# A macaron transformer block on one Trainium2 core: the product with w_o by two sets of seven block products, x read back in two lots, one load pool for all stages

## The chip, the cores and the metric

One NeuronCore of one Trainium2 chip runs the whole kernel in one launch. The metric is the device time in microseconds; the time before is the median of three runs, 1166.94 us (1165.9 to 1168.38). All operands are fp32, 512 tokens by 1024 features.

## The reference, cut to what matters

The block is two feed-forward networks with a mixer between them; the change is in the last lines of the mixer.

```python
x = x + 0.5 * swiglu(rmsnorm(x, g1), ffn1_w_gu, ffn1_w_down)
x = x + hybrid_mixer(rmsnorm(x, gm), ...)
x = x + 0.5 * swiglu(rmsnorm(x, g2), ffn2_w_gu, ffn2_w_down)
return rmsnorm(x, final_norm_g)

# the end of hybrid_mixer
y_conv = (cb * causal_short_conv(cc * cu, conv_w)) @ w_out_conv    # 1024 x 1024
y_gla = (o * silu(r)) @ w_out_gla                                  # 1024 x 1024
merged = sigmoid(ga) * y_conv + sigmoid(gb) * y_gla
return merged @ w_o                                                # 1024 x 1024
```

## The kernel before, in words

**Layout.** Activations are held transposed: eight tiles of 128 features by 512 tokens. TensorE takes a 128 x 128 block of a weight matrix as the loaded operand and streams 512 or 256 tokens past it. An fp32 product is made of three passes in the type fp32r: high part of the weight by high part of the activation, high by low, low by high. The high part is a cast, the low part what is left of the value after subtracting the cast.

**Weights.** `Weights` walks a table. `PLAN` lists every block of every weight matrix in the order in which it lies in DRAM; `STEPS` lists what TensorE does with it, step by step. A block of 128 x 1024 values is loaded by SyncE (`dma`, L334) into one of ten load slots `f`; `until` notes the step after which a slot is free. For each step, ScalarE casts the block into `wh` (L374) and VectorE subtracts into `wl` (L375); there are three buffers of each, and a step's cast and subtraction are issued two steps ahead of its matmuls, so the cast of step k waits for the buffer that the matmuls of step k-3 read.

**Sets of seven products.** Wide matrices are not multiplied block by block. A 2 x 2 arrangement of blocks is done with seven products in place of eight, by sums and differences of blocks on both sides (as Strassen's method does). The products are named m1, p2, q6, p5, q7, p4, p3. Each takes one sum of weight blocks and one sum of activation blocks: 24 matmuls of 128 x 256 on TensorE (L533, class `Product`, `narrow`). The sums of weight blocks are made in the load slots: VectorE adds one (L361), and the others are added by GpSimd DMAs that add into their target (L352, `add`). The first of these, a11 += a21, is issued when m1's low part is done, the second, a12 += a11, when p2's is. `sets` puts the blocks of a matrix into `PLAN` and the order of the products into `STEPS`; where two sets follow each other, `order` interleaves them: 0:m1 p2 q6 p5 q7, 1:m1, 0:p4 p3, 1:q6 p5 q7 p2 p4 p3. The sums of the activation side (`Operands`) are VectorE operations of 128 x 1024 in place (L749 to L756); each operand is then split by ScalarE casts (L623) and VectorE subtractions (L624) into two `op` tiles, of which there are 14. `run_sets` asks for operands two steps ahead.

**Accumulation.** A set needs three PSUM banks, a, b and c. Bank b is read after m1, q6 and q7, into a tile or another bank (ScalarE, L579 and L583), and is accumulated into further. When a quarter of the output is complete (p2, q7, p4, p3), VectorE takes it out: for w_out_gla, it is multiplied by a gate (L1641) and added to the merged tiles y (L1645).

**The stage of the change.** After w_out_conv (eight plain units, one of eight 128-column stripes each) comes w_out_gla, two sets, 14 products, 336 matmuls of 128 x 256. Then the four merged y tiles are split (L1560 and L1561, four times, 128 x 1024 each), and w_o is multiplied plainly: four steps that make four stripes at once (`mm_group`, L423, 96 matmuls of 128 x 512), then four single stripes (`mm_single`, L409, 96 more). `evac` adds each stripe to the old x (L1662, eight of 128 x 512) and starts that stripe's part of the next norm (L459 to L469). The old x was written to DRAM earlier; eight SyncE DMAs (L1623) read it back during w_out_conv into tiles that are free by then, and the sum goes into the tile X2. FFN2 follows with plain steps.

**Order.** All of the code is written in one sequence and a scheduler places each engine's instructions; what stands in each engine's list is what the engine runs, in that order. PSUM banks of the pool `mm` are handed out in turn; `AUX` is a bank apart.

Of the kernel before, what the change touches and what calls it, by code (L numbers as in the profile page):

```python
# [8 lines left out]
F32 = mybir.dt.float32  # L9
# [6 lines left out]
P = 128  # L16
# [55 lines left out]

HW = 256


# [104 lines left out]
def block_kernel(ctx: ExitStack, tc: tile.TileContext, xT, vecs, gf, gup, wgl, wts, out):  # L180
# [98 lines left out]
    for n, b in (("wh", 3), ("wl", 3), ("op", 14)):  # L279
        pools[n] = ctx.enter_context(tc.tile_pool(name=n, bufs=b))  # L280
    acc_row = ctx.enter_context(tc.tile_pool(name="acc_row", bufs=1))
    class Weights:

        def __init__(self, ahead):
            self.ahead = ahead
            self.issued = 0
            self.taken = 0
            self.end = 0  # L290
            self.ready = []
            self.raw = {}
            self.loads = {}
            self.sums = {}
            self.first = {}

        def phase(self, early, first=6):


            self.early = early  # L300
            self.until = [-1] * SLOTS
# [27 lines left out]
        def dma(self, n, until):  # L329
            u = PLAN[n]  # L330
            w = unit_cols(u)
            o = offset(n)
            t = self.slot(until)
            nc.sync.dma_start(t[:, :w], wts[o : o + P * w].rearrange("(p n) -> p n", p=P))  # L334
            return t

        def load_set(self, n):

            a = {p: STEPS.index((n, p)) for p in SEQ}
            for i in range(self.issued, a["m1"]):  # L340
                if STEPS[i][1] is None and STEPS[i][0] not in self.raw:
                    self.raw[STEPS[i][0]] = self.dma(STEPS[i][0], i)
            a21 = self.dma(n + 2, max(a["p5"], a["m1"] + 3))
            a11 = self.dma(n, a["p2"] + 3)
            a22 = self.dma(n + 3, a["p4"])
            s3 = self.slot(a["q7"])
            a12 = self.dma(n + 1, a["p3"])
            self.raw[n] = [a11, a12, a21, a22, s3]
# [5 lines left out]
        def issue(self):  # L354
# [192 lines left out]
    class Set:  # L547
# [52 lines left out]
        def quarter(self, p):  # L600
# [12 lines left out]
            return t  # L613

    class Both:

# [113 lines left out]
    class Operands:  # L730
# [4 lines left out]

        def __init__(self, b):
            self.b = b
            self.parts = {}
            self.sums = set()
# [20 lines left out]
        def make(self, p):  # L760
            if p in self.parts:
                return
            i = self.ORDER.index(p)
            if i > 0:
                self.make(self.ORDER[i - 1])
            v = self.sum(p)
# [377 lines left out]
    def mixer(norm, nxt):  # L1144
# [8 lines left out]

        Y = [tile_of("y", [P, 2, S + 2]) for _ in range(4)]

# [422 lines left out]
        def sigmoid(t):  # L1578
# [3 lines left out]

        c_h, c_l = parts([Y[i][:, :, 2:] for i in range(4)])
        m = [two(d // 2)[:, d % 2] for d in range(KD)]

# [9 lines left out]
        ga = [gate("ga", d) for d in range(2)]  # L1595
        x_old = [QK[2 + i][:, j] for i in range(2) for j in range(2)] + [
            pools["g"].tile([P, S], F32, tag=t, name=f"{t}_x") for t in ("sc", "reset", "gup_w", "glr")]
        gb_new = []
# [5 lines left out]
        for d in range(KD):  # L1604
# [16 lines left out]
            if d in AT:  # L1621
                oo.make(AT[d])
            nc.sync.dma_start(x_old[d], xs[d])  # L1623
            if d < 4:
# [4 lines left out]
        sigmoid(gb_new.pop())  # L1629
        m_h, m_l = [None] * KD, [None] * KD  # L1630

        def gla_done(i):
            def done(s, p):
                if not (i == 1 and p in ("q6", "p5", "q7")):
                    finish_late()
                if p not in QUARTERS:
# [6 lines left out]
                    op0=ALU.mult, op1=ALU.mult)  # L1643
                y = two(d // 2)
# [12 lines left out]

        run_sets(lambda i: Set(oo, gla_done(i)), hooks={(0, "p3"): [reload]})
        finish_late()
# [5 lines left out]
        for d, o in enumerate(mm_group("w_o", KD, (0, P, 2 * P, 3 * P), m_h, m_l)):  # L1665
            evac(d, o)
        for d in range(4, KD - 2):
            evac(d, mm_single("w_o", KD, d * P, m_h, m_l))
        for d, o in [(d, mm_single("w_o", KD, d * P, m_h, m_l)) for d in range(KD - 2, KD)]:
            evac(d, o)  # L1670

    FFN = dict(f=1, hidw=2, hid=3, tp=9)
    with phase("small1", **FFN):
# [10 lines left out]
        ffn("ffn1_w_gu", "ffn1_w_down", n1, nm, PLAIN1, 5)  # L1684
    with phase("small2", f=1, v=4, qk=2, g=1, y=4, small=1):
        W.phase(4, 5)
# [49 lines left out]
```

## Time and profile before

| what | value |
|---|---|
| median of three runs | 1166.94 us |
| the profiled execution's own time | 1166.18 us |
| its span in the trace | 1164.1 us |
| granted TensorE clock | 0.999 |
| TensorE matmul, busy | 1155.0 us in 6626 matmuls |
| VectorE, busy | 956.7 us in 1198 instructions |
| ScalarE, busy | 684.6 us in 904 instructions |
| GpSimd, busy | 117.7 us in 153 instructions |

How to read it: `PE` is TensorE's matmul row, `PEld` its weight loads, `DVE` VectorE, `ACT` ScalarE, `POOL` GpSimd and `SP` SyncE. A busy PE row is not a measure of throughput, since matmuls overlap each other: the time of one matmul is read from the distance between starts. In the timeline a row gives the start, the length, the line, output<-inputs, the shape and the count. The first 366 us are FFN1, the mixer follows to 823 us (w_out_gla from 739.14 us, w_o from 779.67 us), and FFN2 is the rest.

### The profile page before, as it was taken

How to read it: one execution, taken by the hardware profiler on the slowest of the kernel's cores; microseconds unless marked ns; L12 is line 12 of the kernel's file. 1: busy time of each engine (PE TensorE's matmuls, PEld its weight loads, DVE VectorE, ACT ScalarE, POOL GpSimd, SP SyncE). 2: the span in 40 equal slices, each digit the busy share in tenths (PEclk: the TensorE clock that was granted, in tenths of full speed). 3: DMA queues.
4: the chain of work that ended last, by engine and by line, in shares of the span. 5: the costliest groups of instructions: out<-in, count | busy, mean ns of one | idle time of the engine just before them, and what ended most of it. 6: DMA issues, size and time to landing. Idle time of an engine off the chain costs nothing.

```text
span 1164.1 us, 17143 instructions
## 1 busy us (share of the span) xinstructions
PE 1155.0 (99%) x6626; PEld 1016.1 (87%) x6626; DVE 956.7 (82%) x1198; ACT 684.6 (59%) x904; POOL 117.7 (10%) x153
## 2 busy tenths in 40 slices
PE   9999999999999999999999999999999999999997
PEld 7898888988888889999989998998889888898886
DVE  7997888997568977979799998686599788889955
ACT  6466666675335656666666586544356666666443
POOL 0010111101020111100101100000001111111100
PEclk9999999999999999999999999999999999999999
DMA  9388787678524488876868767531738777757721
GB/s 350 79 212 195 178 201 180 163 193 204 207 80 122 106 200 230 197 188 171 224 169 207 211 171 221 134 107 52 227 74 209 182 187 177 196 145 183 184 86 73
DMA packets 62593, 200.11 MB, mean 172 GB/s; under 512 B 6864, under 2 KB 13136, under 8 KB 62512
## 3 DMA queue, kind: packets, MB, share of 16 engines
q1 hardware_dynamic: 39088, 126.37, 32.3%
q0 software_dynamic: 18784, 68.17, 31.8%
q10 hardware_dynamic: 4640, 4.49, 1.1%
q8 instruction: 52, 0.85, 0.3%
q14 instruction: 29, 0.24, 0.1%
HBM read 124.55 MB, written 8.39 MB: 114 GB/s over the span
## 4 chain that ended last, share of the span: by engine, by line
PE 96%; DVE 2%; ACT 1%; DMA 1%; issue 1%; ACTq 0%
PE mm L824 13%; PE mm L409 11%; PE mm L533 11%; PE bb L542 10%; PE z L542 8%; PE mm L423 8%; PE w L542 7%; PE y L542 6%; PE mm L1041 4%; PE aux L824 4%; PE x L542 3%; PE y L533 3%; PE w L533 2%; PE aux L1041 1%; PE z L533 1%; PE x L533 1%
## 5 line engine op out<-in xcount | busy, mean ns | idle before, releaser
L374 ACT CAST wh<-f 128x1024 fp32r<-128x1024 f32 (+1 forms) x341 | 356.0, 1047 | 339.6 <-PE mm L533 37.8
L375 DVE TENSOR_TENSOR wl<-f,wh 128x1024 fp32r<-128x1024 f32 (+1 forms) x341 | 413.6, 1217 | 98.4 <-ACT wh L374 89.3
L352 POOL DMA_DIRECT2D f<-f x126 | 109.0, 865 | 905.8 <-DVE wl L375 512.0
L824 PE MATMUL mm<-wh,op 128*128 128x512 f32 x432 | 106.9, 389 | 0.0
L533 PE MATMUL mm<-op,wh 128*128 128x256 f32 x800 | 105.6, 284 | 0.0
L533 PEld LDWEIGHTS mm<-op,wh 128*128 128x128 f32 x800 | 100.1, 192 | 0.5 <-ACT tp L583 0.2
L542 PE MATMUL bb<-op,wh 128*128 128x512 f32 x384 | 97.9, 395 | 0.0
L824 PEld LDWEIGHTS mm<-wh,op 128*128 128x128 f32 x432 | 80.9, 188 | 16.7
L409 PE MATMUL mm<-op,wh 128*128 128x512 f32 x384 | 91.0, 389 | 0.0
L409 PEld LDWEIGHTS mm<-op,wh 128*128 128x128 f32 x384 | 72.0, 188 | 15.0
L542 PEld LDWEIGHTS bb<-op,wh 128*128 128x128 f32 x384 | 69.4, 189 | 12.7
L542 PE MATMUL z<-op,wh 128*128 128x512 f32 x256 | 64.4, 393 | 0.0
L423 PE MATMUL mm<-op,wh 128*128 128x512 f32 x256 | 64.1, 392 | 0.2 <-DVE op L456 0.2
L824 PE MATMUL mm<-wl,op 128*128 128x512 f32 x216 | 57.7, 389 | 0.0
L423 PEld LDWEIGHTS mm<-op,wh 128*128 128x128 f32 x256 | 47.5, 188 | 10.9 <-ACT wh L374 0.5
L542 PEld LDWEIGHTS bb<-op,wl 128*128 128x128 f32 x384 | 52.3, 190 | 5.0 <-DVE wl L375 1.3
L533 PE MATMUL mm<-op,wl 128*128 128x256 f32 x400 | 56.5, 283 | 0.0
L542 PE MATMUL w<-op,wh 128*128 128x512 f32 x224 | 56.3, 393 | 0.0
L542 PE MATMUL bb<-op,wl 128*128 128x256 f32 x384 | 53.6, 282 | 0.9 <-DVE wl L375 0.9
L542 PEld LDWEIGHTS z<-op,wh 128*128 128x128 f32 x256 | 46.0, 189 | 8.2
L361 DVE TENSOR_TENSOR f<-f,f 128x1024 f32<-128x1024 f32 x42 | 51.3, 1222 | 1.6 <-DMA f<-wts 0.9
L533 PEld LDWEIGHTS mm<-op,wl 128*128 128x128 f32 x400 | 51.8, 192 | 0.3
(334 smaller groups left out, 2003.7 us busy)
## 6 DMA issues: line engine op xcount, KB each, us to landing
f<-wts SPq DMA_DIRECT2D x219, 512.0 KB, 4.5
f<-f POOLq DMA_DIRECT2D x126, 512.0 KB, 5.2
X<-xT SPq DMA_DIRECT2D x8, 256.0 KB, 5.4
xs<-X POOLq DMA_DIRECT2D x8, 256.0 KB, 2.4
tp<-ga SPq DMA_DIRECT2D x8, 256.0 KB, 5.6
y<-tp SPq DMA_DIRECT2D x7, 256.0 KB, 2.0
ga<-tp ACTq DMA_DIRECT2D x6, 256.0 KB, 3.9
gb<-tp ACTq DMA_DIRECT2D x6, 256.0 KB, 3.9
```

The lines of the kernel that those rows point to most:

```text
L352: return nc.gpsimd.dma_start(out_, a, accum_op=ALU.add).ins
L361: nc.vector.tensor_tensor(out=s3, in0=a11, in1=a21, op=ALU.add)
L374: self.cast = nc.scalar.copy(h[:, :w], raw[:, :w]).ins
L375: nc.vector.tensor_tensor(out=l[:, :w], in0=raw[:, :w], in1=h[:, :w].bitcast(F32), op=ALU.subtract)
L409: nc.tensor.matmul(o, w[:, i * P : (i + 1) * P], a[k], start=j == k == 0, stop=j == 2 and k == kt - 1)
L423: nc.tensor.matmul(o[c], w[:, s : s + P], a[k], start=k == 0 and j == 0, stop=k == kt - 1 and j == 2)
L533: nc.tensor.matmul(o[:, e * HW : (e + 1) * HW], w[:, k * HW + e * P : k * HW + (e + 1) * P], a(k), start=self.fresh and j == k == e == 0, ...
L542: nc.tensor.matmul(o[:, e, :n], w[:, k * HW + e * P : k * HW + (e + 1) * P], a(k), start=self.fresh and k == 0 and w is self.h, stop=k == ...
L824: nc.tensor.matmul(o[t], a(k)[:, t * P : (t + 1) * P], ww[:, i * 512 : (i + 1) * 512], start=fresh and j == k == 0, stop=j == 2 and k == 3 ...
L1041: nc.tensor.matmul(o[t][e], b if j == 1 else a, wl if j == 2 else wh, start=k == K0 and e == 1 and j == 0, stop=k == KF - 1 and j == 2, sk ...
```

## The change

1. **w_o becomes two sets** of seven products, 2 x 7 x 24 = 336 matmuls of 128 x 256, done by a new class `Straight`. It accumulates into banks a, b, c without reading b out in between, except for one ScalarE copy of bank b into bank a after m1. The plain units, the four splits of y and the eight `evac` additions go. Each set's products come in the order of `OUT_SEQ`; those of w_out_gla in that of `GLA_SEQ`, which differs from before in one place: p2 of the second set comes two products earlier, so that q7 and p4 of that set follow each other directly.
2. **The activation side of w_o** is made by `Operands` over the merged tiles, now one tile `YS` that the view `MY` covers: seven operands, each two casts and two subtractions of 128 x 512, and four sums of 128 x 1024.
3. **The weight sums of w_o.** The third sum, a11 + a21, is not made by VectorE: a11 is loaded a second time and a GpSimd DMA adds a21 to it straight from DRAM (`BY_DMA`). For the second set the sums are placed one step ahead of m1, not three.
4. **x is read back into X2 itself** by eight ScalarE DMAs in two lots of four (`read_back`), and each finished quarter is added in place, by twelve VectorE operations of 128 x 2 x 256.
5. **The load pool `f`** is made once and kept through all stages, and `until` with it.

```diff
+BY_DMA = ("w_o",)
...
+GLA_SEQ = ((0, "m1"), (0, "p2"), (0, "q6"), (0, "p5"), (0, "q7"), (1, "m1"), (0, "p4"),
...
-def sets(mat, pairs):
+def sets(mat, pairs, seq=None):
...
-    STEPS.extend(order(firsts))
+    STEPS.extend([(firsts[i], p) for i, p in seq] if seq else order(firsts))
...
-    sets("w_out_gla", [(4 * i * P, (4 * i + 2) * P) for i in range(2)])
-    units(group("w_o", KD, (0, P, 2 * P, 3 * P)))
-    for d in range(4, KD):
-        units(single("w_o", KD, d * P))
+    sets("w_out_gla", [(4 * i * P, (4 * i + 2) * P) for i in range(2)], GLA_SEQ)
+    sets("w_o", [(4 * i * P, (4 * i + 2) * P) for i in range(2)], OUT_SEQ)
...
+    pools["f"] = ctx.enter_context(tc.tile_pool(name="f", bufs=1, reuse_waits="tile"))
...
-                    self.sums.setdefault(max(lo + 3, i - 3), []).append(n)
+                    ahead = 1 if (PLAN[n][0], STEPS[i - 1][1]) == ("w_o", "q6") else 3
+                    self.sums.setdefault(max(lo + 3, i - ahead), []).append(n)
...
-            s3 = self.slot(a["q7"])
+            s3 = self.dma(n, a["q7"]) if PLAN[n][0] in BY_DMA else self.slot(a["q7"])
...
-                nc.vector.tensor_tensor(out=s3, in0=a11, in1=a21, op=ALU.add)
+                if PLAN[n][0] not in BY_DMA:
+                    nc.vector.tensor_tensor(out=s3, in0=a11, in1=a21, op=ALU.add)
                 self.first[n] = self.add(a21, a22)
+                if PLAN[n][0] in BY_DMA:
+                    self.add(s3, self.block(n + 2))
...
+    class Straight:
...
+        def run(self, p):
+            n = self.BANK[p]
+            fresh = n not in self.bank
+            if fresh:
+                self.bank[n] = self.new(n)
+            Product(*W.take(), self.group.get(p), fresh).narrow(self.bank[n])
+            if p == "m1":
+                self.bank["a"] = self.new("a")
+                nc.scalar.copy(self.bank["a"], self.bank["b"])
+            self.done(p, self.bank[n])
...
-            nc.sync.dma_start(x_old[d], xs[d])
...
-                if p in ("p4", "p3"):
-                    def f():
-                        for j, (b, c) in enumerate(split_pair(y)):
-                            m_h[d + j], m_l[d + j] = b, c
-                    late.append(f)
...
-        def evac(d, o):
-            nc.vector.tensor_tensor(out=x[d], in0=o, in1=x_old[d], op=ALU.add)
-            nxt.add(d)
...
+        def read_back(ks):
+            for d in ks:
+                nc.scalar.dma_start(x[d], xs[d])
...
+        mo = Operands(
+            lambda j, l: MY[:, 4 * j : 4 * j + 4, half(l)],
+            ("m1", "p2", "p5", "q6", "q7", "p3", "p4"))
+
+        def out_done(i):
+            def done(p, o):
+                if p == "m1":
+                    return
+                a = int(p in ("p5", "q7", "p4"))
+                l = int(p not in ("p2", "p4"))
+                d = 4 * i + 2 * a
+                v = XS[-1][:, d : d + 2, half(l)]
+                if a:
+                    nc.vector.scalar_tensor_tensor(out=v, in0=pair(o), scalar=-1.0, in1=v,
+                                                   op0=ALU.mult, op1=ALU.add)
+                else:
+                    nc.vector.tensor_tensor(out=v, in0=pair(o), in1=v, op=ALU.add)
+                for k in NORMS.get((i, p), ()):
+                    nxt.add(k)
+            return done
...
+        def out_bank(i):
+            return lambda n: AUX() if (i, n) == (1, "b") else MM()
...
+        run_sets(out_set, hooks={
+            (0, "p3"): [reload], (1, "q6"): [lambda: read_back(range(0, 4))],
+            (1, "p4"): [lambda: read_back(range(4, KD))]})
```

The scheduler turns this into other lists. **The first place is the end of w_out_gla on TensorE.** Before, the last two products of w_out_gla (p4 into one bank, p3 into another) are followed by the first group of w_o:

```order
L533 MATMUL mm_7281<-op_7236,wl_7441 128x256 x4
L533 MATMUL mm_7281<-op_7239,wl_7441 128x256 x4
L533 MATMUL mm_7408<-op_7275,wh_7475 128x256 x4
L533 MATMUL mm_7408<-op_7278,wh_7475 128x256 x4
L533 MATMUL mm_7408<-op_7275,wh_7475 128x256 x4
L533 MATMUL mm_7408<-op_7278,wh_7475 128x256 x4
L533 MATMUL mm_7408<-op_7275,wl_7476 128x256 x4
L533 MATMUL mm_7408<-op_7278,wl_7476 128x256 x4
L423 MATMUL mm_7584<-op_7503,wh_7513 128x512
```

In the changed kernel, at the same place, the first five matmuls of w_o's m1 (bank mm_7590, weights wh_7510) stand ahead of p4 of w_out_gla (bank mm_7262):

```order
L547 MATMUL mm_7262<-op_7150,wl_7403 128x256 x4
L547 MATMUL mm_7262<-op_7153,wl_7403 128x256 x4
L547 MATMUL mm_7590<-op_7504,wh_7510 128x256 x4
L547 MATMUL mm_7590<-op_7507,wh_7510 128x256
L547 MATMUL mm_7262<-op_7217,wh_7443 128x256 x4
L547 MATMUL mm_7262<-op_7220,wh_7443 128x256 x4
```

The first two rows are the end of q7, and the last two the beginning of p4, both in the same bank; the five matmuls of m1 stand between them, and m1's other nineteen follow after p3.

**The second place is ScalarE beside it.** Before, from the cast for the last product but two to the second split of y for w_o (L374 casts of weights, L583 copies of a bank, L1560 casts of y):

```order
L583 COPY tp_7406<-mm_7281 128x512 [waits PE_49]
L374 CAST wh_7440<-f_6982 128x1024 [waits DMAHW1_49,PE_49,Activation_49]
L1560 CAST op_7503<-y_3174 128x1024 [waits DVE_49]
L374 CAST wh_7475<-f_6985 128x1024 [waits DMASW6_49,PE_49,Activation_49]
L583 COPY tp_7468<-mm_7281 128x512 [waits PE_49]
L374 CAST wh_7513<-f_7438 128x1024 [waits DMAHW4_49,PE_49,Activation_49]
```

In the changed kernel (L388 casts of weights, L597 copies of a bank after q7, L659 casts of operands, L648 the new copy of bank b into bank a):

```order
L388 CAST wh_7510<-f_7295 128x1024 [waits PE_49,Activation_49]
L597 COPY tp_7499<-mm_7262 128x512 [waits PE_49]
L388 CAST wh_7551<-f_7301 128x1024 [waits DMAHW7_49,PE_49,Activation_49]
L388 CAST wh_7591<-f_7293 128x1024 [waits DMASW6_49,DVE_49,PE_49]
L659 CAST op_7548<-y_3170 128x2x256 [waits DVE_49]
L659 CAST op_7584<-y_3170 128x2x256
L659 CAST op_7587<-y_3170 128x2x256
L388 CAST wh_7630<-f_7295 128x1024 [waits DMASW3_49,PE_49,Activation_49]
L648 COPY mm_7619<-mm_7590 128x512 [waits PE_49]
```

The copy after q7 (tp_7499) stands behind the cast of m1's weights (wh_7510), and the copy into bank mm_7619 behind the cast of q6's weights (wh_7630).

**The third place is VectorE in the middle of w_o.** Before (L375 low parts of weights, L1662 the sums with old x, L460 and L469 the norm):

```order
L375 TENSOR_TENSOR wl_7651<-f_7543,wh_7650 128x1024 [waits DMAHW7_49,PE_49,Activation_49]
L375 TENSOR_TENSOR wl_7679<-f_7588,wh_7678 128x1024 [waits DMAHW0_49,PE_49,Activation_49]
L1662 TENSOR_TENSOR X_7377<-mm_7584,qk_3178 128x512 [waits PE_49]
L1662 TENSOR_TENSOR X_7377<-mm_7585,qk_3178 128x512 [waits PE_49]
L1662 TENSOR_TENSOR X_7377<-mm_7586,qk_3179 128x512 [waits PE_49]
```

In the changed kernel (L389 low parts, L660 low parts of operands, L1702 and L1705 the sums in X2, L791 a sum of blocks of y):

```order
L389 TENSOR_TENSOR wl_7631<-f_7295,wh_7630 128x1024 [waits DMASW3_49,PE_49,Activation_49]
L660 TENSOR_TENSOR op_7622<-y_3170,op_7622 128x2x256 [waits Activation_49]
L660 TENSOR_TENSOR op_7625<-y_3170,op_7625 128x2x256 [waits Activation_49]
L1705 TENSOR_TENSOR X_7365<-mm_7619,X_7365 128x2x256 [waits DMAHW6_49,DMAHW5_49,PE_49]
L389 TENSOR_TENSOR wl_7661<-f_7435,wh_7660 128x1024 [waits DMAHW2_49]
L1702 SCALAR_TENSOR_TENSOR X_7365<-mm_7659,X_7365 128x2x256 [waits DMAHW1_49,PE_49]
L791 TENSOR_TENSOR y_3170<-y_3170 128x4x256
L389 TENSOR_TENSOR wl_7698<-f_7299,wh_7697 128x1024 [waits DMASW7_49,Activation_49]
```

Between one low part of a weight and the next there are two or three other operations here, each of which waits for what stands in its row.

The eight read-backs of x stand in ScalarE's list among the casts of the third to the eighth product of w_out_gla, both lots close together.

More of the change, by code (lines that the diff above doesn't have):

```diff
@@ L106, in units @@
         PLAN.append(u)
-def sets(mat, pairs):
+GLA_SEQ = ((0, "m1"), (0, "p2"), (0, "q6"), (0, "p5"), (0, "q7"), (1, "m1"), (0, "p4"),
+           (0, "p3"), (1, "q6"), (1, "p2"), (1, "p5"), (1, "q7"), (1, "p4"), (1, "p3"))
+OUT_SEQ = ((0, "m1"), (0, "p2"), (0, "p5"), (0, "q6"), (1, "m1"), (0, "q7"), (0, "p3"),
+           (0, "p4"), (1, "p5"), (1, "q6"), (1, "p2"), (1, "q7"), (1, "p3"), (1, "p4"))
+def sets(mat, pairs, seq=None):
     firsts = []
@@ L329, in dma, with block @@
         def dma(self, n, until):
-            u = PLAN[n]
-            w = unit_cols(u)
+            w = unit_cols(PLAN[n])
+            t = self.slot(until)
+            nc.sync.dma_start(t[:, :w], self.block(n))
+            return t
+        def block(self, n):
+            w = unit_cols(PLAN[n])
             o = offset(n)
-            t = self.slot(until)
-            nc.sync.dma_start(t[:, :w], wts[o : o + P * w].rearrange("(p n) -> p n", p=P))
-            return t
+            return wts[o : o + P * w].rearrange("(p n) -> p n", p=P)
         def load_set(self, n):
@@ L613, in quarter, with __init__ @@
             return t
+    class Straight:
+        BANK = {"m1": "b", "p2": "a", "q6": "b", "p5": "c", "q7": "b", "p4": "b", "p3": "c"}
+        def __init__(self, group_, done, new):
+            self.group = group_
+            self.done = done
+            self.new = new
+            self.bank = {}
+        def run(self, p):
[8 more added lines that the diff above has]
+            self.done(p, self.bank[n])
     class Both:
@@ L734, in block_kernel, with __init__ @@
         ORDER = ("m1", "p2", "p5", "q6", "q7", "p4", "p3")
-        def __init__(self, b):
+        def __init__(self, b, seq=ORDER):
             self.b = b
+            self.seq = seq
             self.parts = {}
@@ L762, in make @@
                 return
-            i = self.ORDER.index(p)
+            i = self.seq.index(p)
             if i > 0:
-                self.make(self.ORDER[i - 1])
+                self.make(self.seq[i - 1])
             v = self.sum(p)
@@ L1151, in mixer @@
             nc.gpsimd.dma_start(xs[k], x[k])
-        Y = [tile_of("y", [P, 2, S + 2]) for _ in range(4)]
+        YS = tile_of("y", [P, 4, 2, S + 2])
+        Y = [YS[:, i] for i in range(4)]
         def flat(i):
@@ L1583, in mixer @@
         c_h, c_l = parts([Y[i][:, :, 2:] for i in range(4)])
-        m = [two(d // 2)[:, d % 2] for d in range(KD)]
+        MY = YS.rearrange("p i e t -> p (i e t)")[:, : KD * S].rearrange("p (d t) -> p d t", t=S)
+        m = [MY[:, d] for d in range(KD)]
         n64 = [front.tile([P, HEADS * 16], F32, tag=t, name=f"{t}o") for t in
@@ L1595, in mixer @@
         ga = [gate("ga", d) for d in range(2)]
-        x_old = [QK[2 + i][:, j] for i in range(2) for j in range(2)] + [
-            pools["g"].tile([P, S], F32, tag=t, name=f"{t}_x") for t in ("sc", "reset", "gup_w", "glr")]
         gb_new = []
@@ L1643, in done @@
                     op0=ALU.mult, op1=ALU.mult)
-                y = two(d // 2)
+                y = MY[:, d : d + 2]
                 nc.vector.tensor_tensor(out=y[:, :, half(l)], in0=y[:, :, half(l)], in1=pair(g),
                                         op=ALU.add)
-                if p in ("p4", "p3"):
-                    def f():
-                        for j, (b, c) in enumerate(split_pair(y)):
-                            m_h[d + j], m_l[d + j] = b, c
-                    late.append(f)
             return done
@@ L1656, in reload, with out_set @@
             x[:] = [XS[-1][:, k] for k in range(KD)]
-        run_sets(lambda i: Set(oo, gla_done(i)), hooks={(0, "p3"): [reload]})
-        finish_late()
-        def evac(d, o):
-            nc.vector.tensor_tensor(out=x[d], in0=o, in1=x_old[d], op=ALU.add)
-            nxt.add(d)
[L1665 to L1672, printed above, removed]
+        def read_back(ks):
[20 more added lines that the diff above has]
+            return done
+        NORMS = {(0, "p3"): (0, 1), (1, "p2"): (2, 3), (1, "p3"): (4, 5), (1, "p4"): (6, 7)}
+        def out_bank(i):
+            return lambda n: AUX() if (i, n) == (1, "b") else MM()
+        def out_set(i):
+            if i < 2:
+                return Set(oo, gla_done(i))
+            return Straight(mo, out_done(i - 2), out_bank(i - 2))
+        run_sets(out_set, hooks={
+            (0, "p3"): [reload], (1, "q6"): [lambda: read_back(range(0, 4))],
+            (1, "p4"): [lambda: read_back(range(4, KD))]})
+    FFN = dict(hidw=2, hid=3, tp=9)
     with phase("small1", **FFN):
@@ L1684, in block_kernel @@
         ffn("ffn1_w_gu", "ffn1_w_down", n1, nm, PLAIN1, 5)
-    with phase("small2", f=1, v=4, qk=2, g=1, y=4, small=1):
+    with phase("small2", v=4, qk=2, g=1, y=1, small=1):
         W.phase(4, 5)
```

5 lines of the change are left out of this document (1 added, 4 removed).

## The prediction

> **What bounds the kernel now.** I read the page first, then the waits of TensorE, the chain that ended last and the timeline of TensorE.
>
> ```profile
> PE 1155.0 (99%) x6626; PEld 1016.1 (87%) x6626; DVE 956.7 (82%) x1198; ACT 684.6 (59%) x904; POOL 117.7 (10%) x153
> PE 96%; DVE 2%; ACT 1%; DMA 1%; issue 1%; ACTq 0%
> PE aux L267 <- POOL ones L264: 1.1, 1, 1.1
> PE bb L542 <- DVE wl L375: 0.9, 1, 0.9
> PE mm L423 <- DVE op L456: 0.2, 1, 0.2
> ```
>
> The chain lies on TensorE for 96% of the span, and its waits in all are 1.1 + 0.9 + 0.2 us. So the time changes only by what TensorE has to do and by new waits of TensorE; the first is read from the distance between starts of its runs, not from its busy share. The chain's rows for the stages around the change (start, length, then what ran):
>
> ```profile
> 739.30 40.53 PE mm L533 x336
> 779.83 21.79 PE mm L423 x96
> 801.62 21.76 PE mm L409 x96
> 823.38 16.33 PE mm L423 x72
> ```
>
> The first row is w_out_gla, two sets of seven products. The next two are w_o, 192 matmuls of 128x512 in 43.55 us: 0.227 us each. In the timeline:
>
> ```profile
> 767.93 2.08 PE L533 MATMUL mm<-op,wh 128*128 128x256 f32 x16
> 769.85 1.12 PE L533 MATMUL mm<-op,wl 128*128 128x256 f32 x8
> 770.81 2.08 PE L533 MATMUL mm<-op,wh 128*128 128x256 f32 x16
> 772.73 1.12 PE L533 MATMUL mm<-op,wl 128*128 128x256 f32 x8
> 773.82 2.17 PE L533 MATMUL mm<-op,wh 128*128 128x256 f32 x16
> 776.79 2.08 PE L533 MATMUL mm<-op,wh 128*128 128x256 f32 x16
> ```
>
> A product of 24 narrow matmuls takes 770.81 - 767.93 = 2.88 us, 0.120 us each. The next one, at 773.82, is late by 773.82 - 770.81 - 2.88 = 0.13 us, and the last at 776.79 - 773.82 = 2.97 by another 0.09: 0.22 in all. Without that, w_out_gla takes 14 x 2.88 = 40.32 us.
>
> **The matmuls.** w_o becomes 336 narrow matmuls, the same count and shape as w_out_gla. If nothing waits, FFN2 starts 28 x 2.88 = 80.64 us after the start of w_out_gla, 739.30 in the chain: at 819.94. Before it started at 823.38. That is 3.44 us less: 43.55 - 40.32 = 3.23, and the 0.22 that should go, since p2 of the second set moves forward and its weight sum is wanted two products later. [...] At half of 0.227 the products would save 43.55 - 336 x 0.1135 = 5.4 us; 2.2 of these are lost to the smaller size, and 3.2 stay.
>
> **New waits at two seams.** Why the 0.22 us were lost shows on ScalarE:
>
> ```profile
> 767.22 1.05 ACT L374 CAST wh<-f 128x1024 fp32r<-128x1024 f32 x1 [1.35 <-issue]
> 772.24 1.05 ACT L374 CAST wh<-f 128x1024 fp32r<-128x1024 f32 x1 [3.02 <-DMA f<-f]
> 773.19 0.58 ACT L583 COPY tp<-mm 128x512 f32<-128x512 f32 x1
> 773.66 1.05 ACT L374 CAST wh<-f 128x1024 fp32r<-128x1024 f32 x1
> ```
>
> TensorE wanted p4's bank, which the copy (773.19 to 773.77) had to read first, and the copy stood behind a cast that had waited for an accumulating DMA. A copy that starts at the right time, but behind a cast, costs TensorE tenths of a microsecond; the change makes two such seams.
>
> *End of w_out_gla.* q7 and p4 now share a bank and follow each other. q7 takes the place at 770.81, and its high part has read its buffer by about 772.9 (the low part starts at 772.73, in the row above; the matmul before it must drain). Only then can the cast of m1's weights run, 1.05 us, to 773.99; m1's first five matmuls, put there to cover the copy, wanted to start at 773.69. The copy, behind that cast, runs 773.90 to 774.48, under the five (5 x 0.120 = 0.6 us). Loss: 0.35, and 0.1 for starting up again as at 773.82 (0.05 after the copy, and a run 0.09 longer): 0.45 us. It is zero if that cast gets its buffer 0.4 us sooner, and 0.9 if the copy isn't covered.
>
> *m1, then p2, in w_o.* p2 adds into a bank that the copy after m1 fills. m1's low part lasts 8 x 0.120 = 0.96 us; the cast of q6's weights gets its buffer when m1's high part is done, takes 1.05, and the copy stands behind it. So it begins about 0.1 us after m1 ends and takes 0.58; with TensorE's restart the seam is some 1.2 us wide. Five matmuls of p5 cover 0.6. Loss: 0.57 us, between 0.1 (the cast goes early) and 1.2.
>
> The second set's m1 has eight matmuls and the whole of q7 behind it; nothing is lost there.
>
> **The last sums by DMA.** The accumulating DMA a12 += a11 now feeds p3, third after p2. The last p4 is due at 739.14 (the timeline's start of w_out_gla) + 27 x 2.88 = 816.9, and with the losses above at about 818.07; p3 a product earlier, at 815.19, and its cast 1.05 before that, at 814.1; p2 at 809.43. p2's low part, in its place in VectorE's list, is ready at about 808.65.
>
> ```profile
> DMA to landing us min/median/max: 4.6/4.8/4.8
> f<-f POOLq DMA_DIRECT2D x126, 512.0 KB, 5.2
> ACT wh L374 <- DMA f<-f: 28.0, 12, 6.1
> ```
>
> The first row is the GpSimd line alone in 735 to 800 us, the second the page's median over all 126. It lands between 813.45 and 813.85, in time by 0.25 to 0.65 us; casts did wait for such DMAs twelve times in this kernel. I take 0.2 us, ends 0 and 1.7. The DMA share is low here:
>
> ```profile
> 752.00:800.00 48.00, 48.00 (x321) 44.34 (x320) 31.40 (x36) 19.39 (x21) 0.86 (x1) 1.00 0.35 96
> ```
>
> (time, then busy us and count of TensorE, weight loads, VectorE, ScalarE, GpSimd, then clock, DMA share, GB/s). [...]
>
> **VectorE.** Gone in w_o: four subtractions of 128x1024 and eight sums of 128x512. New: fourteen subtractions and twelve sums of 128x512, four sums of 128x1024, and w_o has 14 low parts where it had eight.
>
> ```profile
> 777.59 1.22 DVE L375 TENSOR_TENSOR wl<-f,wh 128x1024 fp32r<-128x1024 f32 x1
> 778.72 0.68 DVE L1641 SCALAR_TENSOR_TENSOR g<-mm,g 128x512 f32<-128x512 f32 x1
> 779.33 1.21 DVE L375 TENSOR_TENSOR wl<-f,wh 128x1024 fp32r<-128x1024 f32 x1
> L375 DVE TENSOR_TENSOR wl<-f,wh 128x1024 fp32r<-128x1024 f32 x22 | 26.8, 1220 | 12.9 <-ACT wh L374 12.8
> ```
>
> From start to start a wide one takes 1.13 us and a narrow one 0.61. From m1's low part to the sum that frees q7's bank for the last p4, VectorE's list holds 17 wide and 35 narrow: 19.2 + 21.4 = 40.6 us, in the 44 us from 774 to 818.07. It was busy 31.4 of 48 before, and is now at 92%. Placed one behind the other with their waits, all come in time, the last by nothing: it ends at 818.05. I take 0.1 us; the upper end is the rival below.
>
> **Hidden.** The cast's work on ScalarE rises by 14 x 0.62 - 4 x 1.05 = 4.5 us, the six more weight casts by 6.3, and eight DMA issues at 0.37 by 2.9 (next rows), where 19.4 of 48 us were busy. A read-back that waits holds up the casts behind it, but a cast gets its buffer 2.1 us into the third product before its own, and so has 3 x 2.88 - 2.1 - 1.05 = 5.5 us to spare; beyond that TensorE waits. SyncE loses eight DMAs; two of its longest waits there were for them:
>
> ```profile
> L623 ACT CAST op<-O 128x512 fp32r<-128x512 f32 x5 | 2.7, 615 | 0.0
> L1524 ACTq DMA_DIRECT2D ga<-tp x6: 366/366/413, 437.3 to 506.7; - x6
> SPq L1623 <- DVE g L1284: 6.6, 1, 6.6
> SPq L1623 <- DVE g L519: 1.8, 1, 1.8
> ```
>
> Weight loads stood behind those waits, ahead of TensorE's one wait in the mixer (0.9 us, for VectorE's low part). That wait names a late subtraction, not a late load, so I leave it in place. The pool that now spans all stages only changes which slot a load takes at two stage borders, where TensorE shows no wait: zero, bounds 0.9 on either side.
>
> **Sum.** 3.44 - 0.45 - 0.57 - 0.2 - 0.1 = 2.1 us less. The profiled execution took 1166.18 us (span 1164.1), so 1164.1; the median of the runs shown is 0.76 higher, 1166.94, and from it the forecast is **1164.8**. It is just within 0.2% (2.33 us), about what a measurement of this kernel can tell from no change. Its own range, with one of the seams at an end, is 1164.6 to 1165.7.
>
> **Rivals.**
>
> *A wait that I price is not there.* If either seam is covered (2.6 us less), if both are (3.1 and up to 3.44), or if the stall of 0.9 at 595 us goes with SyncE's waits (3.0), the time is 1163.5 to 1164.4, with two of them 1162.6. For it: the seams hang on tenths of a microsecond. Against: the row at 773.82 shows such a seam costing its tenths.
>
> [...]
>
> *Slower: VectorE sets the pace of w_o.* In the 84 us from 739 to 823 it stood idle 12.9 us ahead of 22 low parts, waiting for their casts: 0.59 each. With 14 in the new stretch that is 8.2 us of idle beside 40.6 of work, 48.8 for 44: 4.7 us late at the last bank, and 2.6 slower in all, **1169.5**. It decides for slower by 0.2% from 3.4 + 2.1 + 2.3 = 7.8 us of idle on. For it: every operation in the list waits for another engine. Against: much of the 12.9 us was VectorE standing ready early, at 65% busy.
>
> *The change doesn't do what it says.* OUT_SEQ could be undone by the scheduler; the lists show that it isn't, except that both lots of x are read back together, which ScalarE's room covers.
>
> **How the numbers follow.** Forecast 0.42, eaten or half eaten 0.11: within 0.2%, 0.53. A wait not there: 0.34, faster. VectorE's pace: 0.13, slower. The range leaves out most of the last case and little on the other side: 1162.5 to 1168.0.
>
> **What would show it.** In the profile after: narrow runs of 2.88 us through w_o, FFN2 starting near 821.2; one gap of TensorE near 773.7 and one near 783.4, each about half a microsecond, released by ScalarE (cast, and copy). Wrong if the waits of TensorE in w_o name VectorE with more than a microsecond, if a cast waits for a read-back of x, or if the runs in w_o are wider than 2.88 without a wait.

## The result, and the profile after

The changed kernel takes 1174.16 us (median of eight runs, 1171.7 to 1179.45) against 1166.35 us for the kernel before in the same runs: a ratio of 1.0066, 95% interval 1.0044 to 1.0088. It is slower, by some 8 us, and the forecast said 1164.8. The ratios in this section and the next are not quotients of these medians, and differ from them by up to 0.14%. The profiled execution took 1173.95 us, its span 1172.2 us.

These are the longest waits of TensorE in the changed kernel, to be set beside the three rows of before (each row: waiting tile and line, what it waited for, total us, times, longest):

```profile
PE mm L547 <- ACT mm L648: 4.4, 1, 4.4
PE y L547 <- ACT tp L726: 1.2, 2, 0.7
PE aux L272 <- POOL ones L269: 1.1, 1, 1.1
PE bb L556 <- DVE wl L389: 0.9, 1, 0.9
PE aux L1427 <- DVE tp L447: 0.6, 1, 0.6
PE aux L547 <- DVE X L1702: 0.6, 1, 0.6
```

The first row is new, and by far the largest: TensorE waits 4.4 us for the copy of bank b into bank a, the seam between m1 and p2 of w_o. In its timeline (start, length, what ran, idle before):

```profile
777.12 2.78 PE L547 MATMUL mm<-op,wh 128*128 128x256 f32 x21 [0.24 <-ACT wh L388]
...
785.86 0.76 PE L547 MATMUL mm<-op,wh 128*128 128x256 f32 x5
791.00 3.63 PE L547 MATMUL mm<-op,wh 128*128 128x256 f32 x16 [4.38 <-ACT mm L648]
794.42 1.20 PE L547 MATMUL mm<-op,wl 128*128 128x256 f32 x8
795.46 1.48 PE L547 MATMUL mm<-op,wh 128*128 128x256 f32 x11
```

p5's five matmuls that should cover the copy end at 786.5, and p2 begins at 791.00. Then its first sixteen matmuls take 3.63 us where sixteen took 2.08 before. The windows around it (time, busy us of TensorE, weight loads, VectorE, ScalarE, GpSimd, granted clock, DMA share, GB/s):

```profile
780.00:786.00 6.00, 6.00 (x53) 6.00 (x52) 5.03 (x8) 3.64 (x5) 1.75 (x2) 1.00 1.03 208
786.50:790.90 4.40, 0.12 (x1) 0.00 (x0) 3.70 (x5) 1.49 (x2) 0.86 (x1) 1.00 0.40 78
791.00:794.60 3.60, 3.60 (x17) 3.60 (x18) 0.71 (x1) 0.00 (x0) 0.00 (x0) 0.53 0.96 247
794.80:800.00 5.20, 5.20 (x45) 5.20 (x45) 3.69 (x6) 3.19 (x5) 0.14 (x1) 1.00 0.39 110
```

For 3.6 us after the wait the granted clock is 0.53. Now ScalarE at that place, then GpSimd's timeline, and the landing times of GpSimd's four DMAs from 776 to 792 us:

```profile
782.82 1.05 ACT L388 CAST wh<-f 128x1024 fp32r<-128x1024 f32 x1 [1.78 <-PE mm L547]
783.77 1.66 ACT L659 CAST op<-y 128x512 fp32r<-128x512 f32 x3
789.41 1.04 ACT L388 CAST wh<-f 128x1024 fp32r<-128x1024 f32 x1 [3.99 <-DMA f<-f]
790.36 0.58 ACT L648 COPY mm<-mm 128x512 f32<-128x512 f32 x1
```

```profile
777.03 0.87 POOL L363 DMA_DIRECT2D f<-wts  x1 [9.46 <-DMA f<-wts]
780.38 1.75 POOL L363 DMA_DIRECT2D f<-f  x2 [2.48 <-DVE y L1677]
```

```profile
DMA to landing us min/median/max: 6.0/6.8/8.4
```

The copy stands behind the cast of q6's weights, as the order showed, and that cast did not wait for its buffer: it stood for 3.99 us until the accumulating DMA a11 += a21 had landed. m1's low part, after which it may be issued, was done at 778.33; GpSimd issued it at 780.92, second of the two at 780.38, since the second set's first sum stood ahead and waited; and it took 8.4 us to land, the longest of the four from 776 to 792 us. The DMA share was 1.03 there; at the same place of the kernel before, six microseconds to 776.50 and six from there, it had been 0.63 and 0.16.

The rest of the time came in other places. By the starts of the matmuls in the two profiles, in us:

| stretch | before | after | difference |
|---|---|---|---|
| up to the first matmul of w_out_gla | 739.14 | 742.17 | +3.0 |
| w_out_gla and w_o | 84.07 | 88.34 | +4.3 |
| FFN2's first matmul to the last matmul | 333.7 | 334.1 | +0.4 |
| last matmul to the end | 7.2 | 7.6 | +0.4 |

The second row is 28 x 2.88 = 80.64 us and 7.7 of losses: 6.1 at the seam m1 to p2 (4.5 waiting, 1.6 at the lower clock), 0.5 at the end of w_out_gla, 0.3 ahead of the last p3 and 0.8 ahead of the last p4.

### The profile page after: what moved, and what is told of

It reads as the page before. It is cut to its first block, busy times and chain, and to the rows that moved or that the text cites. A ratio compares the mean times of both kernels' runs of the same rounds, so it can differ in the third digit from the quotient of the medians.

```text
span 1172.2 us, 17527 instructions
## 1 busy us (share of the span) xinstructions
PE 1155.2 (99%) x6770; PEld 1022.7 (87%) x6770; DVE 973.3 (83%) x1222; ACT 693.8 (59%) x922; POOL 124.4 (11%) x161
## 5 line engine op out<-in xcount | busy, mean ns | idle before, releaser
L388 ACT CAST wh<-f 128x1024 fp32r<-128x1024 f32 (+1 forms) x347 | 361.9, 1047 | 338.4 <-PE mm L547 41.0
L389 DVE TENSOR_TENSOR wl<-f,wh 128x1024 fp32r<-128x1024 f32 (+1 forms) x347 | 420.7, 1216 | 89.9 <-ACT wh L388 81.5
L363 POOL DMA_DIRECT2D f<-f x132 | 114.0, 866 | 890.4 <-DVE wl L389 498.9
L547 PE MATMUL mm<-op,wh 128*128 128x256 f32 x960 | 128.2, 286 | 4.7 <-ACT mm L648 4.4
L547 PEld LDWEIGHTS mm<-op,wh 128*128 128x128 f32 x960 | 121.4, 194 | 5.6 <-ACT mm L648 4.6
L423 PE MATMUL mm<-op,wh 128*128 128x512 f32 x320 | 75.8, 389 | 0.0
L423 PEld LDWEIGHTS mm<-op,wh 128*128 128x128 f32 x320 | 60.0, 188 | 12.5
L547 PE MATMUL mm<-op,wl 128*128 128x256 f32 x480 | 67.8, 283 | 0.0
L547 PEld LDWEIGHTS mm<-op,wl 128*128 128x128 f32 x480 | 62.3, 192 | 0.3
L437 PE MATMUL mm<-op,wh 128*128 128x512 f32 x192 | 48.4, 394 | 0.0
L556 PE MATMUL y<-op,wh 128*128 128x512 f32 x192 | 48.3, 393 | 0.0
```

What stands on the lines that cost most here:

```text
L363: return nc.gpsimd.dma_start(out_, a, accum_op=ALU.add).ins
L388: self.cast = nc.scalar.copy(h[:, :w], raw[:, :w]).ins
L389: nc.vector.tensor_tensor(out=l[:, :w], in0=raw[:, :w], in1=h[:, :w].bitcast(F32), op=ALU.subtract)
L423: nc.tensor.matmul(o, w[:, i * P : (i + 1) * P], a[k], start=j == k == 0, stop=j == 2 and k == kt - 1)
L437: nc.tensor.matmul(o[c], w[:, s : s + P], a[k], start=k == 0 and j == 0, stop=k == kt - 1 and j == 2)
L547: nc.tensor.matmul(o[:, e * HW : (e + 1) * HW], w[:, k * HW + e * P : k * HW + (e + 1) * P], a(k), start=self.fresh and j == k == e == 0, ...
```

## The experiments

Twelve more runs were made, one of them of the kernel before. The table has the medians, and the ratios to the kernel before in the same runs:

| kernel | median us | ratio, 95% |
|---|---|---|
| e1_pool: before, one pool | 1167.02 | 1.0006 (0.9997 to 1.0015) |
| e2_copy: after, copy ahead of the cast | 1169.56 | 1.0030 (1.0018 to 1.0042) |
| e3_sum: after, sum earlier in GpSimd's list | 1170.41 | 1.0037 (1.0024 to 1.0050) |
| e4_both: both mends | 1167.82 | 1.0020 (1.0005 to 1.0034) |
| e5_s3: after, third sums by VectorE | 1170.38 | 1.0021 (1.0004 to 1.0038) |
| e6_seq: e4 with w_out_gla's old order | 1176.24 | 1.0085 (1.0073 to 1.0098) |
| e7_s3both: e4 and e5 | 1167.90 | 1.0006 (0.9995 to 1.0018) |
| e8_s3seq: e7 with the old order | 1173.86 | 1.0070 (1.0057 to 1.0083) |
| e9_nopool: after, a pool per stage | 1171.36 | 1.0044 (1.0030 to 1.0058) |
| e10_best: e7, a pool per stage | 1165.53 | 0.9994 (0.9985 to 1.0003) |
| e11_before: before again | 1166.73 | one run |
| e12_pool2: e7, FFN1's pool apart | 1166.60 | 1.0003 (0.9994 to 1.0012) |

**The copy alone.** Only two entries of ScalarE's list change places, the copies of the two sets and the casts ahead of them.

```diff
-            self.cast = nc.scalar.copy(h[:, :w], raw[:, :w]).ins
+            with ExitStack() if hold is None else tc.issue_after(hold):
+                self.cast = nc.scalar.copy(h[:, :w], raw[:, :w]).ins
...
-                nc.scalar.copy(self.bank["a"], self.bank["b"])
+                W.hold = nc.scalar.copy(self.bank["a"], self.bank["b"]).ins
```

> The changed kernel, with the copy of bank b into bank a placed ahead of the cast of the next product's weights in ScalarE's list, in both sets; nothing else moves. Theory A, the wait of 4.5 us between m1 and p2 is the copy standing behind a cast that waits for an accumulating DMA: the wait falls to 0.6 us, the slow matmuls behind it (1.6 us) go, and the time falls by 5 to 5.5 us to about 1169. Rival, VectorE sets the pace of w_o or the late DMA itself does: the wait moves to the next product, q6, and the time stays above 1173.

It took 1169.56 us, 4.6 less. ScalarE and TensorE's waits in w_o in its profile:

```profile
786.29 0.57 ACT L652 COPY mm<-mm 128x512 f32<-128x512 f32 x1 [0.63 <-PE mm L551]
789.30 2.00 ACT L392 CAST wh<-f 128x1024 fp32r<-128x1024 f32 x2 [2.44 <-DMA f<-f]
```

```profile
PE aux L551 <- DVE X L1706: 0.6, 1, 0.6
...
PE mm L551 <- ACT wh L392: 0.4, 2, 0.2
```

The DMA lands as late as ever (the cast still waits 2.44 us for it), but nobody waits for that cast: q6 is two products away. The 4.4 us are gone from the list, and w_out_gla and w_o take 83.48 us in place of 88.34. So it was the copy's place in the queue that made TensorE wait for the late transfer. The rival, the wait moving on to q6, fell.

**The sum alone.** GpSimd's list alone changes: q6's sum ahead of the second set's.

```diff
-                self.first[n] = self.add(a21, a22)
+                self.first[n] = self.add(a21, a22, self.m1_add if PLAN[n][0] == "w_o" else None)
...
-                self.add(a11, a21, self.first[twin])
+                self.m1_add = self.add(a11, a21, self.first[twin])
```

> The changed kernel, with GpSimd's list altered at one place: the accumulating DMA that q6 of the first set needs stands ahead of the first one of the second set, not behind it. Theory A with the queue as the cause: it is issued 2 us earlier, when m1's low part is ready, and no other lands beside it, so it lands in about 5 us in place of 8.4; the cast is in time, the wait falls to under 1.5 us and the time to about 1170. Rival, the landing is slow by itself and the place in the queue is worth only its 2 us: 1172.

1170.41 us. TensorE waited for the copy still, but 1.1 us:

```profile
PE aux L1429 <- DVE tp L449: 3.2, 1, 3.2
...
PE mm L549 <- ACT mm L650: 1.1, 1, 1.1
```

On the changed kernel's clock the DMA was issued 2.3 us earlier, and landed in 7.4 us in place of 8.4. So of the 3.3 us that went from the wait, the place in the queue was 2.3, and the quicker landing the rest; whether fewer transfers beside it made it quicker, this run does not show alone. The landing that I expected, 5 us, did not come. (The 3.2 us in the first row lie in the mixer's first stage and are taken up below.)

**Both.** 

> The changed kernel with both: the copy ahead of the cast, and the accumulating DMA ahead of the second set's. Theory A: the same seam is mended twice, so the time is that of the copy alone, about 1169, within 0.7. Rival, two separate losses: each adds its own, 1167 or less.

1167.82 us, from 1165.0 to 1173.9. Its interval overlaps that of the copy alone, so the question of one loss or two is not settled by the time. The profile says one: the seam is 0.2 us late in both. Another wait came up, for q7's operands, whose casts stood behind a weight cast:

```profile
PE mm L553 <- ACT op L665: 1.4, 1, 1.4
```

```profile
795.09 1.05 ACT L393 CAST wh<-f 128x1024 fp32r<-128x1024 f32 x1 [4.34 <-DMA f<-f]
796.04 1.13 ACT L665 CAST op<-y 128x512 fp32r<-128x512 f32 x2
```

It is the same mechanism at another place: something that TensorE needs stands behind a cast that waits for an accumulating DMA.

**Fewer transfers.** The third sum of each set goes back to VectorE: two loads and two accumulating DMAs less.

```diff
-BY_DMA = ("w_o",)
+BY_DMA = ()
```

> The changed kernel, with the third sum of each w_o set made by VectorE as in the sets before, so that two loads and two accumulating DMAs of 512 KB go; the copy stays behind the cast, and the accumulating DMA in its place in GpSimd's list. In the changed kernel the DMA that q6 waits for was issued 2.6 us late and took 8.4 us, at a DMA share of 1.03. Theory A, it was slow because of the crowd of transfers: it now lands in 6 us or less, the wait between m1 and p2 falls from 4.5 to 2 us or less with no slow matmuls behind it, and the time falls to 1169 or 1170. Rival, its place in the queue and VectorE's load decide: the wait stays above 3.5 us and the time above 1173.

The DMA landed in 6.7 us, in place of 8.4; the wait for the copy fell to 1.3 us.

```profile
787.37 1.04 ACT L388 CAST wh<-f 128x1024 fp32r<-128x1024 f32 x1 [0.95 <-DMA f<-f]
788.32 0.58 ACT L648 COPY mm<-mm 128x512 f32<-128x512 f32 x1
```

The DMA was also issued sooner, 780.57 - 743.16 = 37.4 us after the start of w_out_gla in place of 38.75. So of the 3.0 us that the cast gained against that start, 1.7 came from the landing and 1.3 from the issue. The crowd of transfers is part of the cause, as far as one profile shows; the 6 us that I asked for were not reached. The time, 1170.38 us with a ratio of 1.0021, is near what theory A said. VectorE, with two more operations of 128x1024 in its list, did not become the bound: TensorE's wait for its sums in X2 was 0.6 us, as in the changed kernel.

**Fewer transfers, with both mends.** 

> The kernel with both mends, and the third sums made by VectorE. With both mends TensorE still waited 1.4 us for q7's operands, whose casts stood behind a weight cast that waited 8.2 us for its accumulating DMA. Theory A, the crowd of transfers: that wait goes, 1166.5 and less spread between runs (it was 1165.0 to 1173.9). Rival, VectorE, at 92% in w_o by my count, can't take 2.3 us more: later waits for it grow, 1168 or more.

The wait for q7's operands went, and w_out_gla and w_o took 82.69 us, 1.4 less than before the change. The median is 1167.90 all the same, between theory A's time and the rival's: the profiled execution had lost 4.3 us before w_out_gla began.

**The old order in w_out_gla.** Both mends, with the old sequence of the products of w_out_gla.

```diff
-    sets("w_out_gla", [(4 * i * P, (4 * i + 2) * P) for i in range(2)], GLA_SEQ)
+    sets("w_out_gla", [(4 * i * P, (4 * i + 2) * P) for i in range(2)])
```

> The kernel with both mends (copy ahead of the cast, accumulating DMA ahead of the second set's; 1167.8 us), with the products of w_out_gla in their old order, so that p2 of its second set stands between q7 and p4 again. Theory A: the seam at the end of w_out_gla (0.5 us) goes and nothing else: 1167.3. Rival, the old order brings back its 0.2 us wait for an accumulating DMA, or pushes w_o's first sums later: 1168 or more.

> The kernel with both mends, the third sums made by VectorE and the old order in w_out_gla. Theory A: both gains add, about 1166, the first version that is not slower than the kernel before (1166.5). Rival, VectorE's load: 1168 or more.

Both expectations failed by far: 1176.24 and 1173.86 us, 8 and 6 more than with the new order. In the first of the two:

```profile
PE mm L553 <- ACT tp L603: 3.0, 1, 3.0
```

```profile
780.58 1.04 ACT L393 CAST wh<-f 128x1024 fp32r<-128x1024 f32 x1 [6.98 <-DMA f<-f]
781.53 0.58 ACT L603 COPY tp<-mm 128x512 f32<-128x512 f32 x1
```

```profile
777.00:782.00 5.00, 2.16 (x19) 1.96 (x17) 0.52 (x2) 1.42 (x2) 0.00 (x0) 1.00 0.94 206
782.20:785.60 3.40, 3.40 (x16) 3.40 (x17) 3.37 (x6) 0.85 (x1) 0.00 (x0) 0.52 0.80 261
```

This is the seam of the kernel before, at which I had read a loss of 0.22 us: the copy after q7 behind a cast that waits for a12 += a11. Before, that DMA was issued 767.37 - 739.14 = 28.2 us after the start of w_out_gla. Here it is issued at 775.20, 30.8 us after its start (744.45), because p2's low part is made later: counted from the start of w_out_gla, its cast ends 1.1 us later than before, and three operations of 128x512 on VectorE (L1679, L666, L1683) stand between the cast and the low part, which begins 1.85 us after the cast's end in place of 0.46. The 2.5 us make a wait of 3.0 us and a stretch at a clock of 0.52. GLA_SEQ, which I had costed at its seam of 0.45 us, is what kept this away.

w_out_gla and w_o took 88.33 us in the profile of e6_seq, 84.28 in that of e4_both, and 89.25 in e8_s3seq for 82.69 in e7_s3both: the old order costs 4.1 and 6.6 us there. The rest of the 8 us of e6_seq lies ahead of w_out_gla, where the lists of the two kernels are the same, and is not the order's doing.

**The pool.** The kernel before with the one pool, and the changed one without it.

```diff
+    pools["f"] = ctx.enter_context(tc.tile_pool(name="f", bufs=1, reuse_waits="tile"))
...
+            self.until = [-1] * SLOTS
...
-            self.until = [-1] * SLOTS
...
-    FFN = dict(f=1, hidw=2, hid=3, tp=9)
+    FFN = dict(hidw=2, hid=3, tp=9)
...
-    with phase("small2", f=1, v=4, qk=2, g=1, y=4, small=1):
+    with phase("small2", v=4, qk=2, g=1, y=4, small=1):
```

> The kernel before with one part of the change alone: one load pool for all stages, its slot table kept. The changed kernel reached the start of w_out_gla 3.0 us later than the kernel before (742.17 against 739.14 us), ahead of all other parts of the change. Theory A, the 3.0 us are the spread of DMA landings from run to run and belong to no part: this kernel takes 1166.4 us, within 0.7. Theory B, the pool costs them by another order of loads at the stage borders: 1169.4 us, and w_out_gla starts at 742 us.

> The changed kernel with its load pool per stage, as before; w_o, its order and both seams are as in the changed kernel. In every profile with the one pool TensorE waited 0.5 to 3.4 us near 461 us for VectorE, which waited for a DMA that had to land (ga<-tp), and w_out_gla started between 740.6 and 745.4 us; in the one profile of before it started at 739.14. Theory A, the pool's other order of loads makes that wait: w_out_gla starts by 739.7 and the time is 1171 to 1172. Rival, it is the spread of DMA landings: it starts at 740.5 or later and the time stays at 1173 to 1175.

> The kernel before once more, for a second profile. Theory A (the pool makes the wait near 461 us): no wait there over 0.3 us, w_out_gla starts at 739.1 to 739.7 us. Rival (spread of DMA landings): a wait there, and a start at 740.5 or later, as in the profiles with the one pool.

e1_pool takes 1167.02 us, which by itself is not told from the kernel before; its profiled execution, at 1168.1, is one of its slower ones, and begins w_out_gla at 741.41 us, near what theory B said. e9_nopool takes 1171.36, 2.8 less than the changed kernel, though the two intervals overlap a little. In the profiles w_out_gla begins at 738.6 to 739.7 us in the five in which FFN1 has a pool of its own (e12_pool2 too), and at 740.6 to 745.4 in the nine others. So a delay goes with the pool; among the nine, though, it varies from 1.5 to 6.3 us, by more than the 3.0 that are to be explained.

In the changed kernel the 3.0 us come in four places: 0.9 at 222.8 us and 0.7 at 300 us, both in FFN1, 0.6 at 437.6 and 0.8 at 463.4, in the mixer. Three of them stand in TensorE's timeline as waits:

```profile
222.80 2.17 PE L547 MATMUL y<-op,wh 128*128 128x256 f32 x16 [0.67 <-ACT tp L726]
437.61 2.11 PE L556 MATMUL bb<-op,wh 128*128 128x512 f32 x8 [0.52 <-ACT tp L603]
463.44 0.50 PE L1427 MATMUL aux<-tp,ones_r 128*128 128x512 f32 x1 [0.58 <-DVE tp L447]
```

The first two are the mechanism of the seam once more, a copy on ScalarE behind a cast of weights that waits for an accumulating DMA:

```profile
221.21 1.05 ACT L388 CAST wh<-f 128x1024 fp32r<-128x1024 f32 x1 [4.67 <-PE x L547]
222.17 0.58 ACT L726 COPY tp<-y 128x512 f32<-128x512 f32 x1
```

The row names TensorE, but the cast begins when the DMA issued at 215.16 has landed, 5.9 us later. In the kernel before, the same DMA was issued at 215.23 and took 4.7 us, and the copy was just in time. It took 4.6 or 4.7 us in all five profiles with a pool for FFN1, 5.6 to 5.9 in five of the nine others, and 4.6 to 5.0 in the other four.

The third wait is for a DMA, ga<-tp. Of VectorE's waits, the changed kernel's, e3_sum's and e9_nopool's:

```profile
DVE tp L447 <- DMA ga<-tp: 0.7, 1, 0.7
```

```profile
DVE tp L449 <- DMA ga<-tp: 3.4, 1, 3.4
```

```profile
DVE tp L446 <- DMA ga<-tp: 0.3, 1, 0.3
```

This wait is in every profile with the one pool, 0.5 to 3.4 us, and TensorE waits behind it. Of the profiles without, the two of before, e10_best and e12_pool2 have none, e9_nopool 0.3.

How the pool does this is not shown. Between the kernel before and e1_pool, the lists of the engines first differ near 294 us, at the border from FFN1 to the mixer, where a cast and some low parts change places and SyncE issues some of its loads earlier; that may account for the 0.7 us at 300 us. Up to there the lists are the same, so the longer landing at 215 us can't come from their order.

**The best of these, and the border to FFN2.** 

> The kernel with both mends and the third sums made by VectorE, and with the load pool per stage. With the one pool, w_out_gla and w_o took 82.69 us in its profile, 1.4 less than before (84.07), but w_out_gla started 4.3 us later, and the time was 1167.9. Theory A, the pool delays the stages ahead: 1165.0, faster than before (1166.4) by what the products of w_o save less the seams that are left. Rival, the spread of DMA landings: 1167 to 1168, as with the one pool.

1165.53 us, ratio 0.9994 (0.9985 to 1.0003): the change with its faults mended is not told from the kernel before; the interval goes from 1.7 us less to 0.3 us more. Of the 3.44 us that its products save, little is left: w_out_gla and w_o take 83.87 us in its profile, 3.2 more than 28 x 2.88. These are its longest waits in the two stages and at FFN2's start; the rest is shorter losses at the seams:

```profile
PE mm L442 <- ACT wh L392: 0.8, 1, 0.8
PE mm L552 <- ACT wh L392: 0.2, 1, 0.2
PE aux L552 <- DVE X L1707: 0.2, 1, 0.2
```

The first is the wait of FFN2's first matmul, 0.9 us in e9_nopool; e7_s3both, the same kernel with one pool, does not have it. The last kernel gives FFN1 a pool of its own and the rest one:

```diff
-    with phase("small1", **FFN):
+    with phase("small1", f=1, **FFN):
```

> The kernel with both mends and the third sums made by VectorE, the load pool apart for FFN1 and one for the mixer and FFN2. Theory A, the one pool costs at the border from FFN1 to the mixer (the wait near 461 us) and gains at the border to FFN2, where with a pool per stage TensorE waited 0.8 to 0.9 us for the first cast: w_out_gla starts by 739.8, FFN2's first matmul waits under 0.3 us, and the time is 1164.5, a microsecond under the kernel with a pool per stage (1165.5). Rival, the border to FFN2 gives nothing in the end: 1165.5, or 1167.9 if the cost lies there.

Half of this came true. w_out_gla began at 738.60, and FFN2's first matmul had no wait. But FFN2 then took 335.1 us from its first to its last matmul's start, not 333.9 as in e10_best, with a wait for a cast in its second product:

```profile
PE mm L866 <- ACT wh L392: 0.6, 1, 0.6
```

1166.60 us: in this profile, what the pool gains at that border it loses later. The times of e10_best and e12_pool2 are not told apart.

## Why the prediction was wrong, step by step

*The matmuls.* Right. Products of 24 run at 2.88 us wherever nothing waits; what w_out_gla and w_o take beyond 28 x 2.88 us, 7.7 in the profile after, is waits, restarts and the lower clock.

*The seam at the end of w_out_gla.* Right in mechanism and size: 0.5 us, predicted 0.45, released by the cast (0.24 in the timeline row of 777.12, the rest its restart).

*m1, then p2.* This is the step that failed. It was the right seam and the right queue, the copy behind the cast of q6's weights, but the term was 0.57 us, at most 1.2, and it measured 6.1. The step says that the cast "gets its buffer when m1's high part is done, takes 1.05, and the copy stands behind it". The cast also needs its operand, a11 += a21, and that came 4.0 us after its buffer and the casts of operands ahead of it. The step put this wait at nothing. I had worked out such a DMA for the last p3, and said there that casts waited for these DMAs twelve times in this kernel; I did not work it out for q6. q6 itself had time, some 13 us from m1's low part (778.33) to its due start; but the copy behind its cast was wanted 8 us after that low part, at 786.5.

Two sizes decided. The price, 4.6 to 4.8 us to land, was read at a DMA share of 0.35, from the stage that the change fills with loads; at 1.03 it was 8.4. And GpSimd's list, in which another set's sum stands ahead, was not weighed: it put the issue off by 2.6 us. As an estimate from these rows: issued at 778.33 and landing in 4.8 us, the DMA would have been done at 783.1, the cast would have followed the operands' casts at 785.4, the copy would have ended near 787, and the loss would have been the predicted half microsecond. The term was also not added up rightly: the parts that the step names, 0.1 and 0.58 us and a restart as at 773.82 of 0.14, make a seam of 0.8 us and not of 1.2.

*The last sums, VectorE.* p3 lost 0.3 (0.2 predicted) and p4 0.8 (0.1 predicted), since p3's DMA held up VectorE's list behind it. Mis-sized by 0.8 in all. The end of 1.7 us that the prediction names for p3 is shown by no run: in the profile after, p3's DMA was issued at 817.40 and landed in 5.3 us, half a microsecond over the 4.8 of before. (p3 is the second product after p2 there, not the third, and 818.07 should have been 817.92 by its own terms; neither moves the result.) The rival of the other sign, VectorE pacing w_o, was not what happened: it is named for 0.6 us of the waits in w_o, and took two more wide operations in e5 and e7 without harm.

*The pool.* I took zero, bounds 0.9. The medians put it at 2.8 us in this kernel (e9_nopool), 2.4 in the mended one (e10_best against e7_s3both) and 0.5 in the kernel before (e1_pool), with intervals that overlap each time. The step failed too: the words "TensorE shows no wait" at the borders were true of before and say nothing of a new order there, and more than half of the 3.0 us came in FFN1, 0.9 of them ahead of the border's first change.

*The read-backs of x.* No cast waits for one in the profile after; no run tried them apart.

In the sum, 2.1 us less became 8 more: 5.5 from the seam, 0.8 from the last sums, 0.4 in FFN2 (most of it a wait of 0.5 us at 1050.2 us for a copy behind a cast), 0.4 behind the last matmul, whose cause is open, and the 3 us ahead of w_out_gla. The seam's cause is shown by e2_copy. A delay like the 3 us goes with the pool in all the profiles, but how it comes about, and its size, stay open.

## What to carry to other kernels

Where an engine runs its list in order, as ScalarE did here, the price of an instruction on the critical path is the latest of all the waits that stand ahead of it in the queue, each operand of each of them, and not the busy time there: 4.4 us of TensorE's time here, for a copy of 0.58 us behind a cast of 1.05 (gone in e2_copy). A transfer's landing time is to be read at the load that the change itself makes (4.6 to 4.8 us at a DMA share of 0.35 before, 8.4 at 1.03 after), and through the list of the engine that issues it (2.6 us there). A reordering that looks like a side matter can be what keeps such a wait away (3.0 us in e6_seq, 3.4 in e8_s3seq): price it by taking it out.

## What the runs showed of the hardware

Long waits of TensorE cost more than their length here. In the fourteen profiles seven of its waits are 2.0 us or longer: 4.4 (the changed kernel), 3.2 (e3_sum), 2.2 and 3.0 (e6_seq), 2.0 (e7_s3both), 3.4 (e8_s3seq) and 4.9 (e9_nopool). Behind the first five the granted clock was lower for a stretch:

| wait | stretch behind it, us | its granted clock | after it |
|---|---|---|---|
| 4.4, the changed kernel | 791.20 to 794.60 | 0.50 | 0.99 to 796.00 |
| 3.2, e3_sum | 465.20 to 469.00 | 0.55 | 1.00 to 473.00 |
| 2.2, e6_seq | 466.00 to 467.80 | 0.50 | 0.92 from 468.00 to 470.00 |
| 3.0, e6_seq | 782.20 to 785.60 | 0.52 | 1.00 from 786.00 to 790.00 |
| 2.0, e7_s3both | 464.08 to 467.47 | 0.50 | 1.00 to 469.00 |

The longest of the shorter waits was 1.5 us (e5_s3); behind it, and behind the 1.4 of e2_copy (463.90 to 467.00), the clock was 1.00. The cost beyond the wait, read from sixteen matmuls that took 3.63 and 3.64 us in place of 2.08, was some 1.6 us both after the 4.4 and after the 3.0. No wait lies between 1.5 and 2.0 us, and the runs do not show why the clock falls.

The rows show the time behind the 2.0 us of e7_s3both, then that behind the 1.5 us of e5_s3 (window, its length, busy us of TensorE, granted clock, DMA share, GB/s):

```profile
463.30:464.06 0.76, 0.76 (x4) 1.00 0.37 131
464.08:467.47 3.39, 3.39 (x17) 0.50 0.44 153
467.49:469.00 1.51, 1.51 (x15) 1.00 0.19 38
```

```profile
464.46:467.80 3.34, 3.34 (x24) 1.00 0.69 202
```
